# A decoder layer on one core: sums of weight panels made by accumulating DMAs in FFN-down, and panel products placed ahead of five waiting small products in the mixers

## The chip, the cores and the metric

The kernel runs on one core of a Trainium2 chip. The metric is the device time of one execution in microseconds (us), the median of several runs. The engines are named as in the profile: PE does the matrix products, ACT (ScalarE) and DVE (VectorE) the element-wise work, POOL is GpSimd, and SP only issues DMAs here.

## The reference

One layer on a residual stream of 256 tokens by 2048 channels, all in fp32. Two mixers read the normed stream through one input projection: a causal pooling mixer and an RWKV-7 time mix with 16 heads of 64. The FFN is a squared-ReLU MLP, 2048 to 8192 and back; a gated embedding and a last norm end the layer. Cut to its frame:

```python
D_MODEL, SEQ, D_FF, D_PLE, R, N = 2048, 256, 8192, 256, 1024, 64

def rms_norm(x, g):
    return x * lax.rsqrt(jnp.mean(x * x, axis=-1, keepdims=True) + 1e-6) * g

def wkv7_scan(r, decay, k, v, a_vec, b_vec):           # one head, over the 256 tokens
    def step(S, inp):
        r_t, w_t, k_t, v_t, a_t, b_t = inp
        sa = jnp.einsum('bhij,bhj->bhi', S, a_t)
        S = S * w_t[:, :, None, :] + sa[..., None] * b_t[:, :, None, :] + v_t[..., None] * k_t[:, :, None, :]
        return S, jnp.einsum('bhij,bhj->bhi', S, r_t)

def reference(x, p, ...):
    z = rms_norm(x, attn_norm) @ w_in                  # 2048 -> pool 1024, r, k, v 1024 each, w 64, a 64, g 160
    zs = token_shift(z[..., 1024:], mu_shift)          # z + (z of the token before - z) * mu
    d = causal_multiscale_pool(z[..., :1024])          # windows 2, 4, 8, 16
    pool_out = jnp.einsum('btgc,gcd->btgd', d, pool_w).reshape(B, T, 1024) * pool_scale
    rwkv_out = rwkv7_time_mix(zs, ...)                 # decay, a, g from small products; kk normed by head; the scan;
                                                       # group norm by head; + sum(r * k * r_k) * v; times g
    x = x + jnp.concatenate([pool_out, rwkv_out], -1) @ w_out
    x = x + jnp.square(jax.nn.relu(rms_norm(x, mlp_norm) @ w_ffn_up)) @ w_ffn_down
    gate = jax.nn.sigmoid(rms_norm(x, ple_norm) @ w_ple_gate)
    x = x + gate * (p @ w_ple_proj)
    return rms_norm(x, final_norm)
```

## The kernel before, in words

**Products.** Each fp32 weight panel (128 rows by 1024 columns, a 512 KB DMA that SP issues, `load_raw`) is split in two: the high half `wh` is a copy to fp32r on ACT, in two 512-wide instructions, and the low half `wl` is a subtraction on DVE, 1024 wide. An fp32 product is three matmuls with the halves (high by high, low by high, high by low), each 128x128 by 128x512 in the big stages. The activations are kept in halves too. `raw`, `wh` and `wl` tiles come from rotating pools, so a split waits until PE has read the tile that stood in its buffer.

**Order.** The program is written in one thread of calls; Tile's scheduler then orders each engine's instructions. A block under `high_priority` is placed as early as its data and buffers let it.

**The stages**, on the profile's clock: the mixers with the input and output projections to about 378 us, then the FFN in two halves of 4096 hidden channels: FFN-up 378 to 558 and FFN-down 558 to 722.5, then FFN-up 722.5 to 901 and FFN-down 901 to 1070, and the gate to the end. FFN-down is four sweeps, `d00`, `d01`, `d10`, `d11`: half by half of the output columns. A sweep adds 16 pairs of panels (`kp` 0 to 15; 256 hidden channels by 1024 columns each) into PSUM banks.

**Squares.** Most pairs are done plainly, 8 products of 128 channels by 128 tokens by 512 columns, which are 24 matmuls. Some pairs, called squares here, are done by a 2-by-2 scheme of the Strassen-Winograd kind: 7 products, 21 matmuls, for which sums of the four weight blocks (a11, a12, a21, a22 of the activations, w11 to w22 of the weights) are needed. The list `SEVEN` has seven squares in a sweep and the last sweep has four. The activations' sums are made in FFN-up (`activation_sums`, L1191); the weights' sums are made on DVE in the sweep (L1269 to L1272, four 512-wide instructions into a tile `td`), and then split: `wad` (w11, L172/L173), and 1024-wide tiles with the suffixes b, c and d (L1240 on ACT, L1241 on DVE). The products' matmuls are L1229 to L1231 (`prod`).

**Mixers.** Between the small products of the time mix stand the input projection's panel products, which are generators in a queue. `steps(n)` advances the queue by n yields (a yield is one or two matmuls), and `fill(us)` by so many us of panel products at the paces written beside the yields. A number in parentheses at a `z_...` call (for `z_zk1(1.33)`) is the same for the fill ahead of that gemm's transposes. So these numbers say how many panel matmuls PE does ahead of a small product. Small products that the change touches: `wagT` (transposes of the low-rank channels, L464), `zkT` of the second head group (transposes of `zk1s`, L498) and `kkn` (L595) behind it, `bsum` (`block_sum` in `rwkv_values`, L523), and `um` and `sm` in the loop over the four chunks c of `rwkv_core` (L854, L863). `gi` is the head group, 0 or 1.

**Norm.** `rms_stat` for the norm ahead of the FFN (`n2`) squares the residual stream in four 1024-wide ACT instructions into a tile with the tag `junk`.

Of the kernel before, what the change touches and what calls it, by code (L numbers as in the profile page):

```python
# [40 lines left out]
def trunk(  # L41
# [251 lines left out]
    def rms_stat(srcs, name):  # L293
        s4 = const.tile([128, 2, 2], F32, tag="s4", bufs=2, name=f"s4_{name}")
        for tt in range(2):
            for hf in range(2):
                junk = fp.tile([128, 1024], F32, tag="junk", bufs=1, name=f"junk_{name}{tt}{hf}")
                nc.scalar.activation(
                    junk, srcs[tt][:, hf * 1024 : (hf + 1) * 1024], AF.Square, accum_out=s4[:, tt, hf : hf + 1]
                )  # L300
# [101 lines left out]
    def head():  # L402
# [42 lines left out]
        steps(1)  # L445
# [327 lines left out]
    def rwkv_values(gi, st, zv):  # L773
# [3 lines left out]
        for tt in range(2):  # L777
# [16 lines left out]
    def rwkv_core(gi, st):  # L794
# [34 lines left out]
        for c in range(4):  # L829
# [18 lines left out]
            fill(1.59 if gi else 1.14)  # L848
# [10 lines left out]
            fill(0.72 if gi else 0.86)  # L859
# [171 lines left out]
    rwkv_k(1, st1, z_zk1(1.33))  # L1031
# [124 lines left out]
    def inv_ms():  # L1156
        ss2 = rms_stat(xr, "n2")
        nc.vector.tensor_scalar(s2, ss2, 1.0 / D, NORM_EPS, op0=ALU.mult, op1=ALU.add)
        nc.vector.reciprocal(s2, s2)

# [27 lines left out]
    SEVEN = (1, 3, 5, 7, 9, 11, 13)  # L1188
    s_slots = (0, 2, 5)

    def activation_sums(box, kp, r):  # L1191

        i = SEVEN.index(kp)
        if i % 2 == 0:
            st = a8(s_slots[i // 2], f"S{kp}", F32R) if i < 6 else fp.tile([128, 1024], F32R, tag="S", name=f"S{kp}")
            box[kp] = box[SEVEN[min(i + 1, len(SEVEN) - 1)]] = st
# [5 lines left out]
        nc.vector.tensor_tensor(s3, a11, a21, op=ALU.subtract)  # L1202
# [3 lines left out]

    def down_sweep(hf, pair, ys, sboxes, hooks=(), between=None, seven=SEVEN):

        nm = f"d{hf}{pair}"
        hooks = dict(hooks)  # L1210
# [21 lines left out]

        def halves_of(src, name, own=False):

            pool, kw = (fp, dict(bufs=2)) if own else (wp, {})
            wh = pool.tile([128, 1024], F32R, tag="graw" if own else "wh", name=f"wh_{name}", **kw)
            wl = pool.tile([128, 1024], F32R, tag="graw" if own else "wl", name=f"wl_{name}", **kw)
# [10 lines left out]
        def add(tt, c, src):  # L1248
            nc.vector.scalar_tensor_tensor(xs(tt, c), src, s2[:, tt : tt + 1], xs(tt, c), op0=ALU.mult, op1=ALU.add)

        for q, kp in enumerate(((0, 2, 1, 4, 3, *range(5, 16)) if hf else (0, 2, 1, 4, 3, 6, 5, 8, 7, 10, 9, 12, 11, 14, 13, 15)) if pair else range(16)):
# [4 lines left out]
            rx, ry = (load_raw(w_down[pair, hf * 32 + 2 * kp + i], 1024, f"{nm}_{kp}_{i}") for i in range(2))  # L1256
            if kp in seven:
# [6 lines left out]
                w11 = wa[:, 0:512], wa[:, 512:1024]  # L1264
                with tc.high_priority(20000):
                    split_sb(*w11, rx[:, 0:512])
                w21, w22 = halves_of(ry, f"{nm}_{kp}b")
                with tc.high_priority(20000):
                    nc.vector.tensor_tensor(t1, rx[:, 512:1024], rx[:, 0:512], op=ALU.subtract)  # L1269
# [220 lines left out]
```

## Time and profile before

| what | before |
|---|---|
| median of 3 runs | 1180.49 us (1180.44 to 1181.11) |
| the profiled execution | 1180.25 us, of it 1178.2 us in the span |
| granted clock | 0.998 |
| PE busy | 1162.5 us, 6419 matmuls |
| DVE busy | 873.3 us |
| ACT busy | 709.3 us |
| POOL busy | 13.7 us |
| DMA | 216.81 MB, 184 GB/s over the span |

A profile's row names an engine, a line of the kernel, an operation and its tiles (out<-in, buffer numbers left out), with its count and its time. Matmuls are pipelined: one of 128x512 shows 0.39 us, while the next starts 0.23 us behind it. In the view by instruction a bracket gives the idle time ahead of an instruction and what ended it.

### The profile page before, as it was taken

The numbers are of one execution on the slowest core, as the hardware profiler recorded it, in microseconds if no ns is written. First come the engines' busy times: TensorE is split into PE (matmuls) and PEld (weight loads), VectorE is DVE, ScalarE is ACT, GpSimd is POOL, SyncE is SP. The second block draws the span as 40 slices with busy tenths as digits, with TensorE's granted clock in tenths as the row PEclk, the third lists the DMA queues.
The fourth block names the chain that finished last, engine by engine and source line by source line (L and its number), as shares of the span: only waits on it lengthen the run. The fifth ranks groups of instructions, "written<-read, shape, count | busy, mean of one in ns | idle before, by whom it ended". The sixth has DMA issues, their size and how long they took to land.

```text
span 1178.2 us, 17287 instructions
## 1 busy us (share of the span) xinstructions
PE 1162.5 (99%) x6419; PEld 973.4 (83%) x6419; DVE 873.3 (74%) x1188; ACT 709.3 (60%) x1309; POOL 13.7 (1%) x73
## 2 busy tenths in 40 slices
PE   8999999999999999999999999999999999999997
PEld 8787777788887888888888888888888888888886
DVE  7786996964656666767988987676668879788543
ACT  7776848676545565555665664555556655568543
POOL 2100000000000000000000000000000000000000
PEclk9999999999999999999999999999999999999999
DMA  7464343354465555555556556555555555767511
GB/s 290 154 202 146 135 140 119 119 179 157 160 203 178 177 182 196 184 192 200 187 204 212 198 202 209 186 191 191 185 195 190 202 205 195 290 233 249 197 56 72
DMA packets 60756, 216.81 MB, mean 184 GB/s; under 512 B 6784, under 2 KB 7552, under 8 KB 60288
## 3 DMA queue, kind: packets, MB, share of 16 engines
q1 hardware_dynamic: 60240, 214.99, 52.5%
q8 instruction: 50, 0.82, 0.3%
q10 hardware_dynamic: 432, 0.73, 0.2%
q14 instruction: 34, 0.28, 0.1%
HBM read 213.59 MB, written 2.10 MB: 183 GB/s over the span
## 4 chain that ended last, share of the span: by engine, by line
PE 96%; ACT 1%; DVE 1%; DMA 0%; issue 0%; SPq 0%; POOL 0%; DVEq 0%; POOLq 0%
PE u_w L1112 20%; PE u_w L1117 10%; PE d_b L1231 7%; PE d_b L1229 7%; PE d_b L1230 7%; PE d_w L1231 2%; PE d_w L1229 2%; PE d_w L1230 2%; PE gt_b L242 2%; PE gt_b L241 2%; PE gt_b L238 2%; PE zk_b L241 1%; PE zk_b L242 1%; PE o_b L241 1%; PE o_b L242 1%; PE zv_b L238 1%
## 5 line engine op out<-in xcount | busy, mean ns | idle before, releaser
L1112 PE MATMUL u_w<-h,wh_u 128*128 128x512 f32 x1024 | 321.9, 395 | 0.0
L167 ACT ACTIVATE wh_u<-raw_u 128x512 fp32r<-128x512 f32 x256 | 147.5, 623 | 160.9 <-issue 98.2
L168 DVE TENSOR_TENSOR wl_u<-raw_u,wh_u 128x1024 fp32r<-128x1024 f32 x128 | 156.6, 1224 | 105.2 <-ACT wh_u L167 103.5
L1117 PEld LDWEIGHTS u_w<-h,wl_u 128*128 128x128 f32 x1024 | 192.4, 188 | 45.4
L1117 PE MATMUL u_w<-h,wl_u 128*128 128x256 f32 x1024 | 201.4, 278 | 0.0
L1112 PEld LDWEIGHTS u_w<-h,wh_u 128*128 128x128 f32 x1024 | 156.0, 189 | 0.1
L168 DVE TENSOR_TENSOR wl_gt<-raw_gt,wh_gt 128x1024 fp32r<-128x1024 f32 x24 | 29.4, 1224 | 23.2 <-ACT wh_gt L167 23.2
L167 ACT ACTIVATE wh_gt<-raw_gt 128x512 fp32r<-128x512 f32 x48 | 28.0, 638 | 23.1 <-PE gt_b L242 14.4
L241 PE MATMUL gt_b<-wh_gt,h 128*128 128x512 f32 x96 | 37.3, 389 | 0.0
L242 PE MATMUL gt_b<-wh_gt,h 128*128 128x512 f32 x96 | 37.3, 389 | 0.0
L168 DVE TENSOR_TENSOR wl_o<-raw_o,wh_o 128x1024 fp32r<-128x1024 f32 x16 | 19.6, 1222 | 12.9 <-ACT wh_o L167 9.9
L167 ACT ACTIVATE wh_o<-raw_o 128x512 fp32r<-128x512 f32 x32 | 18.4, 623 | 16.3 <-issue 8.5
L167 ACT ACTIVATE wh_zp<-raw_zp 128x512 fp32r<-128x512 f32 x32 | 18.6, 623 | 15.7 <-PE zp_b L242 7.2
L168 DVE TENSOR_TENSOR wl_zk<-raw_zk,wh_zk 128x1024 fp32r<-128x1024 f32 x16 | 19.4, 1220 | 10.4 <-ACT wh_zk L167 10.4
L241 PE MATMUL zk_b<-wh_zk,hTh 128*128 128x512 f32 x64 | 25.2, 394 | 1.4 <-ACT wh_zk L167 1.4
L241 PE MATMUL zv_b<-wh_zv,hTh 128*128 128x512 f32 x64 | 26.0, 406 | 0.0
L167 ACT ACTIVATE wh_zk<-raw_zk 128x512 fp32r<-128x512 f32 x32 | 18.4, 622 | 12.4 <-PE zv_b L242 4.0
L241 PE MATMUL zp_b<-wh_zp,hTh 128*128 128x512 f32 x64 | 25.7, 401 | 0.0
L238 PE MATMUL gt_b<-wl_gt,h 128*128 128x512 f32 x96 | 25.7, 389 | 0.0
L168 DVE TENSOR_TENSOR wl_zv<-raw_zv,wh_zv 128x1024 fp32r<-128x1024 f32 x16 | 19.4, 1218 | 8.2 <-ACT wh_zv L167 7.4
L241 PE MATMUL zr_b<-wh_zr,hTh 128*128 128x512 f32 x64 | 25.4, 397 | 0.0
L242 PE MATMUL zp_b<-wh_zp,hTl 128*128 128x512 f32 x64 | 25.0, 391 | 0.0
(840 smaller groups left out, 2963.9 us busy)
## 6 DMA issues: line engine op xcount, KB each, us to landing
raw_u<-in_w_ffn_up_dram SPq DMA_DIRECT2D x128, 512.0 KB, 3.5
raw_d<-in_w_ffn_down_dram SPq DMA_DIRECT2D x128, 512.0 KB, 4.3
raw_gt<-in_w_ple_gate_dram SPq DMA_DIRECT2D x24, 512.0 KB, 3.5
raw_zk<-in_w_in_dram SPq DMA_DIRECT2D x16, 512.0 KB, 3.7
raw_zr<-in_w_in_dram SPq DMA_DIRECT2D x16, 512.0 KB, 3.3
raw_zv<-in_w_in_dram SPq DMA_DIRECT2D x16, 512.0 KB, 3.3
raw_zp<-in_w_in_dram SPq DMA_DIRECT2D x16, 512.0 KB, 3.2
raw_o<-in_w_out_dram SPq DMA_DIRECT2D x16, 512.0 KB, 4.2
```

What stands on the lines that cost most here:

```text
L167: nc.scalar.activation(wh[:, a * 512 : (a + 1) * 512], raw[:, a * 512 : (a + 1) * 512], AF.Copy)
L168: nc.vector.tensor_tensor(wl, raw, wh.bitcast(F32), op=ALU.subtract)
L238: nc.tensor.matmul(banks[tt], ah[:, ts_], halves[a][1], start=False, stop=last)
L241: nc.tensor.matmul(banks[tt], ah[:, ts_], halves[a][0], start=i + a == 0, stop=False)
L242: nc.tensor.matmul(banks[tt], al[:, ts_], halves[a][0], start=False, stop=False)
L1112: nc.tensor.matmul(bank[:, ct, :].rearrange("p (s t) -> p s t", s=2), wh[:, cs[ct]], hl, start=k == 0, stop=False, skip_group_check=True,)
L1117: nc.tensor.matmul(bank[:, ct, 0:T], wl[:, cs[ct]], hl[:, 0, :], start=False, stop=k == 15, skip_group_check=True)
L1229: nc.tensor.matmul(banks[n], ah, wh, start=first, stop=False)
L1230: nc.tensor.matmul(banks[n], ah, wl, start=False, stop=False)
L1231: nc.tensor.matmul(banks[n], al, wh, start=False, stop=last)
```

## The change

In **FFN-down**, `SEVEN` has eight squares, and the last sweep five: 29 squares in place of 25. The panels of `w_ffn_down` lie in another order in DRAM (on the host). The sum of two weight blocks is now made by DMA: `begin_sum` has GpSimd issue a plain 256 KB DMA of one block into a slot of a two-slot tile `ring`, and then a 256 KB DMA of the other that adds to what is there (`accum_op`). The square's second panel load is 256 KB in place of 512 KB. DVE then makes the remaining sums in two instructions, of 512 and of 1024 elements. The first two sums are begun in FFN-up, and each square's end begins one further sum. The product order within a square is 1, 2, 3, 5, 6, 4, 7 (it was 1, 2, 3, 5, 7, 6, 4), and the visiting order of pairs differs in the sweeps of the second column half. Each fourth pair of split tiles has buffers of its own (`half_tiles`), `wad` lies in `junk`, and the squares of the norm's statistic in the tag `S`. Some sums have the opposite sign, so the last additions use `ns2`, the negative of `s2`.

In the **mixers**, five numbers are larger: `steps(7)` ahead of the norm and `wagT`, 1.90 for `z_zk1`, a `fill` of 0.92 ahead of `bsum` of group 0, and for chunk 0 of group 0 a fill of 1.59 ahead of `um` and one of 1.76 ahead of `sm`.

```diff
@@ rms_stat
-                junk = fp.tile([128, 1024], F32, tag="junk", bufs=1, name=f"junk_{name}{tt}{hf}")
+                junk = fp.tile([128, 1024], F32, tag="S" if name == "n2" else "junk", bufs=1, name=f"junk_{name}{tt}{hf}")
@@ head
-        steps(1)
+        steps(7)
@@ rwkv_values
+        fill(0.00 if gi else 0.92)
         bon = st["rk"]
@@ rwkv_core, chunk c
-            fill(1.59 if gi else 1.14)
+            fill(1.59 if gi or c == 0 else 1.14)
             ub = rw_bank("um")
...
-            fill(0.72 if gi else 0.86)
+            fill(0.72 if gi else 0.86 if c else 1.76)
             if c < 3:
@@ main thread
-    rwkv_k(1, st1, z_zk1(1.33))
+    rwkv_k(1, st1, z_zk1(1.90))
@@ FFN
-    SEVEN = (1, 3, 5, 7, 9, 11, 13)
+    SEVEN = (1, 3, 4, 6, 8, 9, 11, 13)
...
+        squares_of[hf, pair] = (1, 3, 6, 9, 11) if last else SEVEN
...
+    def begin_sum():
+        n = len(begun)
+        if not ring:
+            ring.append(fp.tile([128, 1024], F32, tag="S", name="ring"))
+        if n < len(in_line):
+            hf, pair, kp = in_line[n]
+            nc.gpsimd.dma_start(slot(n), w_down[pair, hf * 16 + kp, 1, :, 1, :])
+            nc.gpsimd.dma_start(slot(n), w_down[pair, hf * 16 + kp, 0, :, 1, :], accum_op=ALU.add)
+            begun.append(n)
@@ down_sweep, a square
-                t_ = a8(1, f"t{nm}_{kp}")
-                t1, t3, t2, t4 = (t_[:, c * 512 : c * 512 + 512] for c in range(4))
-                wa = fp.tile([128, 1024], F32R, tag="wa", name=f"wa{nm}_{kp}")
+                p1 = summed(hf, pair, kp)
+                t2 = p1
+                wa = fp.tile([128, 1024], F32R, tag="junk", bufs=1, name=f"wa{nm}_{kp}")
...
-                    split_sb(*w11, rx[:, 0:512])
-                w21, w22 = halves_of(ry, f"{nm}_{kp}b")
-                with tc.high_priority(20000):
-                    nc.vector.tensor_tensor(t1, rx[:, 512:1024], rx[:, 0:512], op=ALU.subtract)
-                    nc.vector.tensor_tensor(t3, ry[:, 512:1024], rx[:, 512:1024], op=ALU.subtract)
-                    nc.vector.tensor_tensor(t2, t3, rx[:, 0:512], op=ALU.add)
-                    nc.vector.tensor_tensor(t4, ry[:, 0:512], t2, op=ALU.subtract)
-                w1, w3 = halves_of(t_[:, 0:1024], f"{nm}_{kp}c")
-                w2, w4 = halves_of(t_[:, 1024:2048], f"{nm}_{kp}d", True)
+                    split_sb(*w22, ry[:, 0:512])
+                    split_sb(*w1, p1)
+                    nc.vector.tensor_tensor(t2, p1, ry[:, 0:512], op=ALU.subtract)
+                    t43 = rx.rearrange("p (r n) -> p r n", r=2)
+                    nc.vector.tensor_tensor(t43, t43, t2.unsqueeze(1).to_broadcast([128, 2, 512]), op=ALU.subtract)
+                    split_sb(*w2, t2)
+                w4, w3 = halves_of(rx, f"{nm}_{kp}d", True)
...
+                begin_sum()
@@ ffn_half
+            if f in (3, 4):
+                begin_sum()
```

The change of order, at three places. First the head of the mixers, on PE: `sbank` is the norm's sum of squares, `wagT` the transposes that need the norm, and `zk0` the panel product that runs beside them. Before:

```order
L238 MATMUL zk0_b0_216<-wl_zk0_5_487,hTh1_157 128x512
L441 MATMUL sbank_173<-ones_90,sqx1_370 128x1
L441 MATMUL sbank_173<-ones_90,sqx3_495 128x1
L441 MATMUL sbank_173<-ones_90,sqx1_370 128x1
L441 MATMUL sbank_173<-ones_90,sqx3_495 128x1
L238 MATMUL zk0_b1_217<-wl_zk0_5_487,hTh1_157 128x512
L464 MATMUL wagT_518<-ident_85,wagS_515 128x128 x2
L465 MATMUL wagT2_519<-ident_85,wagS_515 32x128
```

After:

```order
L238 MATMUL zk0_b1_217<-wl_zk0_5_487,hTh1_157 128x512
L238 MATMUL zk0_b0_216<-wl_zk0_5_487,hTh1_157 128x512
L238 MATMUL zk0_b1_217<-wl_zk0_5_487,hTh1_157 128x512
L241 MATMUL zk0_b0_216<-wh_zk0_6_517,hTh1_157 128x512
L242 MATMUL zk0_b0_216<-wh_zk0_6_517,hTl1_159 128x512
L241 MATMUL zk0_b1_217<-wh_zk0_6_517,hTh1_157 128x512
L242 MATMUL zk0_b1_217<-wh_zk0_6_517,hTl1_159 128x512
L241 MATMUL zk0_b0_216<-wh_zk0_6_517,hTh1_157 128x512
L242 MATMUL zk0_b0_216<-wh_zk0_6_517,hTl1_159 128x512
L241 MATMUL zk0_b1_217<-wh_zk0_6_517,hTh1_157 128x512
L242 MATMUL zk0_b1_217<-wh_zk0_6_517,hTl1_159 128x512
L464 MATMUL wagT_535<-ident_85,wagS_532 128x128 x2
```

Ten more panel matmuls stand between the norm's sum and `wagT`. The same place on ACT, where `rs_n1` is the square root of the norm and `wagS` the scaled copy that `wagT` transposes, one for each half of the tokens. Before:

```order
L167 ACTIVATE wh_zr0_0_584<-raw_zr0_0_582 128x512 x2
L450 ACTIVATE rs_n1_175<-sbank_173,eps_n_79 128x2
L459 ACTIVATE wagS_515<-wag_b0_169,rs_n1_175 128x288
L459 ACTIVATE wagS_515<-wag_b1_170,rs_n1_175 128x288
L335 ACTIVATE zf_176<-wagT_518,omu_154 128x256
```

After:

```order
L167 ACTIVATE wh_zr0_0_584<-raw_zr0_0_582 128x512 x2
L450 ACTIVATE rs_n1_175<-sbank_173,eps_n_79 128x2
L459 ACTIVATE wagS_532<-wag_b0_169,rs_n1_175 128x288
L167 ACTIVATE wh_zr0_1_622<-raw_zr0_1_620 128x512 x2
L459 ACTIVATE wagS_532<-wag_b1_170,rs_n1_175 128x288
L335 ACTIVATE zf_176<-wagT_535,omu_154 128x256
```

A panel's split now stands between the two halves of `wagS`. On DVE, where the reciprocal of the norm stands behind the panels' low halves, before:

```order
L144 TENSOR_SCALAR oka_155<-par_sb_77 128x8
L145 SCALAR_TENSOR_TENSOR cen_101<-jsum_92,ident_85 128x128
L168 TENSOR_TENSOR wl_zk0_7_561<-raw_zk0_7_558,wh_zk0_7_560 128x1024
L451 RECIPROCAL rs_n1_175<-rs_n1_175 128x2
L133 TENSOR_TENSOR wband_153<-wband_153,ident_85 128x128
```

After:

```order
L145 SCALAR_TENSOR_TENSOR cen_101<-jsum_92,ident_85 128x128
L168 TENSOR_TENSOR wl_zk0_6_518<-raw_zk0_6_515,wh_zk0_6_517 128x1024
L168 TENSOR_TENSOR wl_zk0_7_561<-raw_zk0_7_558,wh_zk0_7_560 128x1024
L168 TENSOR_TENSOR wl_zr0_0_585<-raw_zr0_0_582,wh_zr0_0_584 128x1024
L451 RECIPROCAL rs_n1_175<-rs_n1_175 128x2
```

One more low half, `wl_zr0_0`, stands ahead of the reciprocal. The third place is the begin of FFN-up on ACT: `h2` are the normed, transposed activations, `wh_u...` the panels of FFN-up, `junk_n2...` the squares of the norm's statistic. Before:

```order
L167 ACTIVATE wh_u00_2_3799<-raw_u00_2_3797 128x512 x2
L1140 ACTIVATE h2_3359<-h2t_3731,par_sb_77 128x256 x2
L167 ACTIVATE wh_u00_3_3822<-raw_u00_3_3820 128x512 x2
L1140 ACTIVATE h2_3359<-h2t_3731,par_sb_77 128x256 x2
L167 ACTIVATE wh_u01_0_3852<-raw_u01_0_3850 128x512 x2
L167 ACTIVATE wh_u01_1_3875<-raw_u01_1_3873 128x512 x2
```

After:

```order
L167 ACTIVATE wh_u00_2_3800<-raw_u00_2_3798 128x512 x2
L298 ACTIVATE junk_n201_4166,s4_n2_4163<-x0_2733 128x1024
L298 ACTIVATE junk_n210_4168,s4_n2_4163<-x1_2734 128x1024
L1141 ACTIVATE h2_3359<-h2t_3731,par_sb_77 128x256
L298 ACTIVATE junk_n211_4170,s4_n2_4163<-x1_2734 128x1024
L167 ACTIVATE wh_u00_3_3823<-raw_u00_3_3821 128x512 x2
L1141 ACTIVATE h2_3359<-h2t_3731,par_sb_77 128x256
L167 ACTIVATE wh_u01_0_3853<-raw_u01_0_3851 128x512 x2
L1141 ACTIVATE h2_3359<-h2t_3731,par_sb_77 128x256 x2
L172 ACTIVATE wh_d00_1b_5475<-ring_4590 128x512
L167 ACTIVATE wh_u01_1_3876<-raw_u01_1_3874 128x512 x2
```

Three of the squares, and the split of the first transferred sum (`wh_d00_1b<-ring`, a square of the first FFN-down sweep), now stand in ACT's row here. DVE's row has the matching subtraction `wl_d00_1b<-ring` ahead of `wl_u01_1`.

More of the change, by code (lines that the diff above doesn't have):

```diff
@@ L1205, in activation_sums, with slot, summed, down_sweep @@
         split_sb(st[:, 0:512], st[:, 512:1024], t_[:, 0:512])
-    def down_sweep(hf, pair, ys, sboxes, hooks=(), between=None, seven=SEVEN):
+    ring = []
+    squares_of = {}
+    visits_of = {}
+    for hf in range(2):
+        for pair in range(2):
+            last = hf + pair == 2
+            squares_of[hf, pair] = (1, 3, 6, 9, 11) if last else SEVEN
+            visits_of[hf, pair] = (0, 2, 1, 4, 3, *range(5, 16)) if last else (range(16), (0, 2, 1, 5, 3, 4, 7, 6, 10, 8, 9, 12, 11, 14, 13, 15))[pair]
+    in_line = [(*hp, kp) for hp, visits in visits_of.items() for kp in visits if kp in squares_of[hp]]
+    begun = []
+    turns = []
+    def slot(n):
+        return ring[0][:, n % 2 * 512 : n % 2 * 512 + 512]
+    def begin_sum():
[7 more added lines that the diff above has]
+            begun.append(n)
+    def summed(*square):
+        return slot(in_line.index(square))
+    def down_sweep(hf, pair, ys, sboxes, hooks=(), between=None):
         nm = f"d{hf}{pair}"
+        seven, visits = squares_of[hf, pair], visits_of[hf, pair]
         hooks = dict(hooks)
@@ L1255, in down_sweep @@
             a11, a21, a12, a22 = ((y[:, j + i * 128 : j + i * 128 + 128], y[:, 1024 + j + i * 128 : 1152 + j + i * 128]) for i in range(4))
-            rx, ry = (load_raw(w_down[pair, hf * 32 + 2 * kp + i], 1024, f"{nm}_{kp}_{i}") for i in range(2))
+            rx, ry = (panel(kp, c, f"{nm}_{kp}_{c}", 1 if c and kp in seven else 2) for c in range(2))
             if kp in seven:
```

54 lines of the change are left out of this document (32 added, 22 removed).

## The prediction

> **What bounds the kernel now.** I read the page first: PE is busy for nearly the whole span, and the chain that ended last runs on PE.
>
> ```profile
> PE 1162.5 (99%) x6419; PEld 973.4 (83%) x6419; DVE 873.3 (74%) x1188; ACT 709.3 (60%) x1309; POOL 13.7 (1%) x73
> PE 96%; ACT 1%; DVE 1%; DMA 0%; issue 0%; SPq 0%; POOL 0%; DVEq 0%; POOLq 0%
> ```
>
> So time is won by fewer matmuls, or by PE waiting less, and lost where another engine makes PE wait. The windows by stage (columns: stretch, its length, then busy time and instructions of PE, PEld, DVE, ACT, POOL, then clock, DMA share, GB/s) tell what a matmul is worth, and what stands beside it:
>
> ```profile
> 153.00:165.00 12.00, 10.99 (x58) 8.69 (x57) 11.94 (x23) 5.85 (x12) 1.08 (x2) 1.00 0.35 124
> 378.00:558.00 180.00, 179.44 (x1034) 156.65 (x1034) 124.46 (x159) 99.07 (x180) 0.00 (x0) 1.00 0.55 188
> 558.00:722.50 164.50, 164.50 (x727) 136.21 (x727) 143.51 (x163) 98.72 (x171) 0.00 (x0) 1.00 0.57 201
> 901.00:1070.00 169.00, 169.00 (x756) 139.52 (x755) 144.93 (x165) 104.94 (x188) 0.00 (x0) 1.00 0.63 226
> ```
>
> In FFN-down PE never rests: 164.50 / 727 = 0.2263 us for each matmul. DVE is next, 143.51 of 164.50, so 21 us in two sweeps are free on it. In FFN-up, one matmul in the mean takes 180 / 1034 = 0.174 us. In the mixers DVE can be fuller than PE (11.94 of 12.00). Then PE's waits, all that the view has:
>
> ```profile
> PE zk_b L241 <- ACT wh_zk L167: 1.4, 1, 1.4
> PE rbank L400 <- DVE ones L98: 1.2, 1, 1.2
> PE bsum L523 <- DVE zr_t L336: 1.0, 1, 1.0
> PE sm L863 <- ACT UV L858: 0.9, 1, 0.9
> PE wagT L464 <- POOL wband L130: 0.8, 1, 0.8
> PE zkT L498 <- ACT zk1s L488: 0.8, 2, 0.6
> PE h2t L1134 <- DVE x L1071: 0.6, 1, 0.6
> PE um L854 <- ACT R L818: 0.4, 1, 0.4
> ```
>
> Five of these are the change's places: wagT, zkT, bsum, um, sm. None lies in FFN-down, so there only the count of matmuls can gain.
>
> **FFN-down: fewer matmuls.** Four more squares, each 7 products in place of 8, three matmuls a product: 4 x 3 x 0.2263 = **-2.7 us**. That holds if DVE and ACT still keep ahead. Rows of a square before, on DVE and ACT:
>
> ```profile
> L1269 DVE TENSOR_TENSOR td<-raw_d 128x512 f32<-128x512 f32 x24 | 16.6, 691 | 1.5 <-DMA raw_d<-in_w_ffn_down_dram 0.9
> L1241 DVE TENSOR_TENSOR wl_d_1c<-td,wh_d_1c 128x1024 fp32r<-128x1024 f32 x4 | 4.9, 1220 | 0.7 <-ACT wh_d_1c L1240 0.7
> L172 ACT ACTIVATE wad<-raw_d 128x512 fp32r<-128x512 f32 x24 | 14.8, 618 | 3.7 <-DMA raw_d<-in_w_ffn_down_dram 3.7
> ```
>
> A square now has on DVE four 512-wide instructions (three low halves, one sum) and three 1024-wide (two low halves, one sum): 4 x 0.69 + 3 x 1.22 = 6.4 us, where it had 5 x 0.69 + 3 x 1.22 = 7.1. A plain pair has 2 x 1.22 = 2.4. A sweep of eight and eight is 8 x (6.4 + 2.4) = 70 us on DVE. On ACT a square has seven 512-wide copies and a pair four: 8 x 11 x 0.62 = 55. PE has 8 x (21 + 24) x 0.2263 = 81.5. PE stays the bound; if that cover were gone, each us on DVE would be one on PE. The two further sums of activations for each half, some 2 us of DVE and ACT, fall in FFN-up, where DVE is busy 124 of 180 us: nothing. The tight place is where two squares are neighbours (3, 4 and 8, 9, six times in all): the last split tiles have two buffers, so the second square's last splits start when PE has left the first. From the rows I find 0.2 to 0.7 us to spare, and take 0; the bound is 0.6 each, 3.6 in all.
>
> **FFN-down: the sums by DMA.** No GpSimd DMA and none that adds stands in the trace. The nearest rows of issue to landing, both for 256 KB, and the panels' own:
>
> ```profile
> wa<-in_wa_up_dram SPq DMA_DIRECT2D x2, 256.0 KB, 2.7
> gu<-in_g_up_dram SPq DMA_DIRECT2D x2, 256.0 KB, 4.2
> raw_d<-in_w_ffn_down_dram SPq DMA_DIRECT2D x128, 512.0 KB, 4.3
> ```
>
> The adding DMA waits for the plain one, so a sum takes 5.4 to 8.4 us by the first two rows; I take 7, in the middle. It may take as long as its slot is free. A slot serves every second square; between those lie at the least two squares and a pair on PE, (42 + 24) x 0.2263 = 14.9 us. The old sum is read last by the square's last split, some 6.4 us of DVE behind its begin, the new one some 2.5 us behind the begin of its own: 14.9 - 6.4 + 2.5 = 11 us. So 7 is hidden, by 4 us. On POOL nothing else waits behind these DMAs; on SP the panel's second load shrinks to half. If the cover is gone, each us over 11 comes to PE at up to 27 squares (29 less the two begun in FFN-up).
>
> By the Trainium skill, "DMA: Bandwidth & Descriptors", section "Anatomy of one DMA — SWDGE (gpsimd) path", such a DMA takes about 2.0 us plus its bytes at 436 GB/s, so 256 KB some 2.6 us and a sum 5.2, an estimate; by it this term is 0 as well, with 6 us to spare, and no row here shows it.
>
> **The new wait in FFN-up.** ACT now has the first sum's split in its row ahead of `wh_u01_1`, the sixth panel, and DVE likewise. Behind it are queued every further panel of FFN-up, for which PE waits.
>
> ```profile
> 377.23 1.15 ACT L167 ACTIVATE wh_u<-raw_u 128x512 fp32r<-128x512 f32 x2 [1.38 <-issue]
> 379.89 0.47 ACT L1140 ACTIVATE h<-h2t,par_sb 128x256 fp32r<-128x256 f32 x1 [1.50 <-PE h2t L1134]
> 378.71 0.69 PE L1112 MATMUL u_w<-h,wh_u 128*128 128x512 f32 x2
> L298 ACT ACTIVATE junk_n<-x 128x1024 f32<-128x1024 f32 x8 | 8.6, 1073 | 0.0
> ```
>
> The ring's tile comes free when the last square of the norm's statistic is done. On ACT these stand behind the copy that ends at 378.4: three of 1.07 us and a 0.5 us copy between, 382.1, and I add 0.5 for the start of each. From 382.6, landing is 5.4 to 8.4 us later, 388.0 to 391.0. PE starts FFN-up at 378.7 and reaches the sixth panel after five of 16 x 0.174 = 2.8 us and eight transposes of 0.11 between, at 393.5. Ahead of that lie the ring's split (0.62), the panel's copy (1.15) and its low half (1.22, needed 0.4 us late): the limit is about 390.9. I take 0, since the middle of the bounds lies 1.4 us ahead of it; bounds 0 and +2 (an issue that costs GpSimd a further us or two). The squares themselves move from a later place in FFN-up to here, 3.2 us of ACT; ACT waited 1.38 and 1.50 us there, and the last `h2` copy is needed some 1 us after it would be done: 0.
>
> **Mixers.** The rows at the five places, in time order:
>
> ```profile
> 35.93 1.15 ACT L167 ACTIVATE wh_zr<-raw_zr 128x512 fp32r<-128x512 f32 x2 [0.89 <-PE zk_b L242]
> 36.78 0.48 PE L238 MATMUL zk_b<-wl_zk,hTh 128*128 128x512 f32 x1
> 37.47 0.89 ACT L459 ACTIVATE wagS<-wag_b,rs_n 128x288 f32<-128x288 f32 x2 [0.23 <-DVE rs_n L451]
> 38.08 0.20 PEld L464 LDWEIGHTS wagT<-ident,wagS 128*128 128x128 f32 x2 [1.14 <-POOL wband L130]
> 127.65 0.39 PE L242 MATMUL zr_b<-wh_zr,hTl 128*128 128x512 f32 x1
> 128.60 0.33 PE L498 MATMUL zkT<-ident,zk1s 128*128 128x128 f32 x1 [0.56 <-ACT zk1s L488]
> 129.18 0.98 PE L498 MATMUL zkT<-ident,zk1s 128*128 128x128 f32 x7 [0.25 <-ACT zk1s L488]
> 58.06 0.64 PE L595 MATMUL kkn<-tF_t,jhead 128*32 128x256 f32 x8
> 134.64 2.13 PE L595 MATMUL kkn<-tF_t,jhead 128*32 128x256 f32 x8
> 159.46 0.30 PEld L523 LDWEIGHTS bsum<-ybuf,jsum 128*128 128x128 f32 x2 [1.17 <-PE vt L780]
> 191.64 0.86 PE L238 MATMUL zv_b<-wl_zv,hTh 128*128 128x512 f32 x3
> 192.91 0.27 PE L854 MATMUL um<-R,SC 64*64 64x64 f32 x1 [0.41 <-ACT R L818]
> 195.30 0.40 PE L242 MATMUL zv_b<-wh_zv,hTl 128*128 128x512 f32 x1
> 195.93 0.59 ACT L858 ACTIVATE UV<-um 64x512 f32<-64x512 f32 x1
> 196.57 0.69 PE L863 MATMUL sm<-UV,BKt 128*64 128x64 f32 x16 [0.88 <-ACT UV L858]
> ```
>
> - **wagT**: PE waits 1.14 us. Ten panel matmuls (2.27 us) now run first, which would hide it, but ACT and DVE are reordered too. The low half `wl_zr0_0` now ahead of the reciprocal needs a buffer that PE leaves after three matmuls from 36.78, at 37.6; with 1.22 us it ends at 38.9, the reciprocal at 39.05. Then the first `wagS` (0.45 to 0.5) to 39.6, `wh_zr0_1` (1.15, its buffer left by PE's last `wh_zk0_6` matmul at 39.4) to 40.65, the second `wagS` to 41.1. PE has nothing else from 39.3, less 0.3 for the first transposes: it waits 1.5. **+0.4** (bounds -1.1 and +0.8).
> - **zkT and kkn**: The matmul of 127.65 gives way at 127.88, so PE waits 0.72, then 0.47 (129.18 - 128.60, less the transpose itself). Three more matmuls (0.68) fill the first; the second stays, since `zk1s` does not end sooner. Behind it, `kkn` took 2.13 us where group 0's, in 58.06's row, took 0.64; it now stands later against ACT's squares of `zk`, and I take a third of the 1.5. **-1.2** (0 to -2.2).
> - **bsum**: six matmuls, 1.36 us, into a wait of 1.17: **-1.2** (0 to -1.2).
> - **um, sm**: The rows' last panel matmuls give way at 192.32 and 195.53, so PE waits 192.91 - 192.32 = 0.6 and 196.57 - 195.53 = 1.0. Three matmuls more in front of each; `UV` ends where it did, at 196.5, since ACT's row between is unchanged. Six matmuls, 1.36 us, go into waits: **-1.3** (-1.6 to 0).
>
> The panel matmuls put ahead are missing at the ends of their gemms, where the queue is simply shorter. Mixers: 0.4 - 1.2 - 1.2 - 1.3 = **-3.3**.
>
> **The sum.** -2.7 + 0 + 0 - 3.3 = -6.0. The profiled execution took 1180.25 us, so 1174.25; the median is 0.24 above it: **1174.5 us**.
>
> **The rivals.**
>
> - *All five waits go*: 1.14 + 1.19 + 1.17 + 1.6 = 5.1, and half of kkn's 1.5, so -2.7 - 5.9: **1171.9**. For it: PE's own rows have enough matmuls. Against it: the reordered reciprocal at wagT.
> - *The mixers give nothing back*: DVE is full there (11.94 of 12.00), so what PE gains at one product it waits at the next, whose inputs come no sooner. Then -2.7 alone: **1177.8**. For it: DVE stands in the chain of zr_t, kkn and bsum; against it: three waits name ACT, which is busy 5.85 of 12.00 there.
> - *The neighbouring squares stall*: +3.6, so **1178.1**.
> - *Slower: the DMA sum outlasts its slot.* If a sum takes over 11 us, the square's first split waits on ACT and DVE, then PE, at up to 27 squares. At 11.6 us it is 27 x 0.6 = 16 on top of -6.0: **1190**. It turns slower than before from 11.25 us. A way to it is that GpSimd can't write the DMA's descriptors while DVE works; DVE is busy 143.51 of 164.50. Against it: it would need 4 us more than the middle of my rows. The Trainium skill, "SBUF — State Buffer", has this as 'The "DVE blocks DMA" trap (SWDGE)': while DVE runs a two-port mode, GpSimd is locked out and the DMA waits. By that rule a sum could start only between DVE's instructions, 0.7 to 1.2 us late each time; that alone doesn't reach 11 us, and no row here shows the lock.
>
> **How the numbers follow.** Forecast 0.58, all five 0.12, nothing back 0.15, neighbours 0.05, slower 0.10. A measurement of this kernel tells about 0.2%, 2.4 us, from no change: faster is below 1178.1, which holds the first two, most of the third and half of the fourth, 0.84; same 0.06; slower 0.10. The range leaves out the slower rival and a tail at each end: 1171.5 to 1178.8.
>
> **What would show it.** In the profile after: 12 fewer matmuls; 29 sums by DMA, none over 11 us; each half's FFN-down shorter by 1.4 us (two squares more) and PE without a wait there; wagT still in the list of waits at about 1.5 us, bsum and um gone from it, sm and zkT at 0.4 to 0.5 us. The forecast is wrong if ACT or DVE wait for `ring` in FFN-down, if PE waits near 390 us, or if the mixers end less than 2 us sooner.

## The result: slower, and the profile after

| what | before | after |
|---|---|---|
| median of 7 runs each | 1180.49 us (1179.66 to 1181.53) | 1185.39 us (1183.96 to 1190.19) |
| after to before | | 1.0053, interval 1.0031 to 1.0074 |
| the profiled execution | 1180.25, span 1178.2 | 1185.39, span 1183.3 |
| PE enters FFN-up at | 378.71 us | 383.35 us |
| FFN-down, first half: first to last matmul | 164.39 us | 163.01 us |
| FFN-down, second half | 168.53 us | 167.46 us |

The forecast was 1174.5, in a range of 1171.5 to 1178.8. The kernel is slower by about 0.5%. The page of after, the engines and the chain that ended last:

```profile
PE 1162.4 (98%) x6407; PEld 971.4 (82%) x6407; DVE 878.0 (74%) x1194; ACT 713.7 (60%) x1323; POOL 56.8 (5%) x131
PE 91%; DVE 4%; ACT 2%; DMA 2%; issue 1%; SPq 0%; DVEq 0%; ACTq 0%
```

PE does the twelve matmuls fewer (6407), but is busy just as long, and PE's part of the chain fell from 96% to 91%: DVE, ACT and DMA now set the pace in places. The windows of the two FFN-down stages, cut at their matmuls (columns as in the prediction):

```profile
565.40:728.40 163.00, 163.00 (x721) 134.97 (x721) 146.57 (x162) 101.77 (x179) 23.00 (x32) 1.00 0.77 235
907.00:1074.40 167.40, 167.06 (x746) 138.16 (x745) 149.07 (x167) 106.72 (x193) 15.80 (x22) 1.00 0.77 251
```

FFN-down does what was forecast: no rest for PE in the first half, one of 0.3 us in the second (ahead of the gate), and 1.4 and 1.1 us less than before. The loss lies ahead of it. The waits of PE in after, longest first:

```profile
PE kkn L595 <- ACT tF_t L585: 2.1, 2, 1.1
PE sc L669 <- ACT UV L783: 1.5, 1, 1.5
PE sm L864 <- ACT UV L859: 1.3, 1, 1.3
PE u_w L1113 <- ACT wh_u L167: 1.3, 1, 1.3
PE rbank L400 <- DVE ones L98: 1.2, 1, 1.2
PE u_w L1118 <- DVE wl_u L168: 1.0, 1, 1.0
PE wag_b L393 <- ACT wagh L379: 0.9, 1, 0.9
PE wagT L464 <- ACT wagS L459: 0.9, 1, 0.9
```

`bsum` left the list, as planned, but `kkn`, `sc` and two matmuls of FFN-up (`u_w`) entered it, and `sm` waits longer. With the stages this gives the span: +4.6 in the mixers, +2.9 in the first FFN-up, -1.4 and -1.1 in the two FFN-down stages, together +5.0 of the 5.1. One execution of the mixers is good to 1 or 2 us only: in the five traces whose mixers are those of before, PE enters FFN-up between 377.72 and 380.14.

**The clock.** The granted clock tells a second part:

| kernel | runs | with a mean clock of 0.998 or more | median of these | median of the rest |
|---|---|---|---|---|
| before (beside the experiments) | 91 | 62 | 1180.1 us | 1181.5 us |
| after | 7 | 2 | 1184.0 us | 1189.5 us |

So at full clock the change costs some 4 us, and it makes executions with a lower clock more frequent. (In every trace the clock is 0.50 for the last 3 to 6 us, where PE has next to nothing to do. The nine of the fourteen traces with a mean of 0.998 or more have no other drop; the five with 0.996 or less have one or two.) Where the clock fell in the profiled one shows in the windows around `kkn` (the column after POOL is the clock):

```profile
133.00:137.00 4.00, 1.91 (x10) 0.89 (x10) 3.90 (x10) 2.70 (x7) 0.00 (x0) 1.00 0.40 130
137.00:141.00 4.00, 3.95 (x12) 2.03 (x13) 3.53 (x12) 3.67 (x7) 0.00 (x0) 0.57 0.64 231
```

PE is busy 1.91 of the first 4 us, and in the next 4 the clock is 0.57 in the mean: it is 0.50 for 3.41 us, from 137.15, and full around that. At half the clock PE loses at most half of 3.41, 1.7 us, and the mean over the execution falls by 0.0014 (estimates from these numbers). The traces with the mixers of before agree: the three without a drop enter FFN-up at 377.72 to 378.71, and the two that have one, at 38.1 and 38.6 us (the late split and the plain second DMA), at 379.87 and 380.14. By the same sum the three runs of after at 0.994, some 6 us over the two at 0.998, had about three drops each (an estimate too).

### The profile page after: what moved, and what is told of

It is laid out like the page before. It is cut to its first block, busy times and chain, and to the rows that moved or that the text cites. A ratio compares the mean times of both kernels' runs of the same rounds, so it can differ in the third digit from the quotient of the medians.

```text
span 1183.3 us, 17405 instructions
## 1 busy us (share of the span) xinstructions
PE 1162.4 (98%) x6407; PEld 971.4 (82%) x6407; DVE 878.0 (74%) x1194; ACT 713.7 (60%) x1323; POOL 56.8 (5%) x131
## 4 chain that ended last, share of the span: by engine, by line
PE 91%; DVE 4%; ACT 2%; DMA 2%; issue 1%; SPq 0%; DVEq 0%; ACTq 0%
PE u_w L1113 19%; PE u_w L1118 10%; PE d_b L1261 7%; PE d_b L1262 7%; PE d_b L1263 7%; PE d_w L1263 2%; PE d_w L1261 2%; PE d_w L1262 2%; PE gt_b L238 2%; PE gt_b L241 2%; PE gt_b L242 2%; PE o_b L241 1%; PE o_b L242 1%; PE o_b L238 1%; PE zr_b L241 1%; PE zr_b L238 1%
## 5 line engine op out<-in xcount | busy, mean ns | idle before, releaser
L1231 POOL DMA_DIRECT2D ring<-in_w_ffn_down_dram x29 | 16.6, 574 | 622.8 <-DVE r L1357 190.5
L172 ACT ACTIVATE wad<-ring 128x512 fp32r<-128x512 f32 x29 | 18.2, 628 | 43.5 <-DVE ring L1312 43.5
L1314 DVE TENSOR_TENSOR raw_d<-raw_d,ring 128x1024 f32<-128x1024 f32 x29 | 35.5, 1222 | 0.7
L1232 POOL DMA_DIRECT2D ring<-in_w_ffn_down_dram x29 | 25.2, 869 | 101.5 <-DMA ring<-in_w_ffn_down_dram 101.5
L168 DVE TENSOR_TENSOR wl_zv<-raw_zv,wh_zv 128x1024 fp32r<-128x1024 f32 x16 | 19.5, 1221 | 10.8 <-ACT wh_zv L167 10.8
```

The lines of the kernel that those rows point to most:

```text
L168: nc.vector.tensor_tensor(wl, raw, wh.bitcast(F32), op=ALU.subtract)
L1232: nc.gpsimd.dma_start(slot(n), w_down[pair, hf * 16 + kp, 0, :, 1, :], accum_op=ALU.add)
L1314: nc.vector.tensor_tensor(t43, t43, t2.unsqueeze(1).to_broadcast([128, 2, 512]), op=ALU.subtract)
```

## The experiments: which part loses, and why

The theory from the two traces had three parts: (a) each panel product that is put ahead drags work of DVE or ACT, or a PSUM bank, ahead of the next small product, so PE waits there; (b) the first sum lands too late for FFN-up; (c) FFN-down gains 2.7 us. The rivals: the sums by DMA slow the sweeps, the clock alone makes the difference, or 29 squares are not worth their extra work. Each run was timed in 3 or 5 rounds against before, on one of three chips, and the ratio is to before on the same chip. Before's median was 1180.23 us beside the FFN part alone, the mixer part alone, the late split and zk1 alone; 1180.27 beside the other single numbers and zk1 with the held low half; and 1180.75 beside the bank, the plain second DMA, the fewer squares and the whole change with the late split.

### The FFN part alone

The five mixer numbers are those of before:

```diff
-        steps(7)
+        steps(1)
-        fill(0.00 if gi else 0.92)
-            fill(1.59 if gi or c == 0 else 1.14)
+            fill(1.59 if gi else 1.14)
-            fill(0.72 if gi else 0.86 if c else 1.76)
+            fill(0.72 if gi else 0.86)
-    rwkv_k(1, st1, z_zk1(1.90))
+    rwkv_k(1, st1, z_zk1(1.33))
```

> The changed kernel with the five mixer numbers of before. Theory A (the mixers lost 4.6 us by reordered splits; in FFN-up the first sum's split made every panel behind it wait for the DMA, 2.7 us; FFN-down itself gained 2.7): mixers end as before, PE waits about 2.7 us in FFN-up's sixth panel, total 1180.5 us, the same as before. Rival B (the sums by DMA cost time all over the sweeps, by traffic or by DVE locking GpSimd out): over 1182 us, with waits of ACT and PE in FFN-down. Rival C (the first sum's wait comes only with the mixers' delay): 1178.

Measured: 1182.56 us (12 runs, 1180.01 to 1184.29), ratio 1.0015 [1.0007, 1.0023]. The FFN part alone doesn't gain either. The waits of PE in this kernel's FFN-up:

```profile
PE u_w L1112 <- ACT wh_u L167: 1.8, 1, 1.8
PE u_w L1117 <- DVE wl_u L168: 1.0, 1, 1.0
```

These waits show 2.8 us, and FFN-up as a whole is longer by more: 182.5 us from its first to its last matmul, against 179.1 in before. These 3.4 us take the 2.7 that FFN-down gives. The median lies in rival B's range, but its mechanism isn't there: PE's list of waits names none in FFN-down, and FFN-down has its gain. The next experiment but one tests that.

### The mixer part alone

Before, with the five numbers of the change.

> The kernel before with the five mixer numbers of the change. Theory A: FFN-up starts 4.6 us later than before, so about 1185 us, and the granted clock falls near 138 us. Rival B (the mixers lose nothing by themselves): 1177 to 1180.

Measured: 1184.91 us (6 runs), 1.0042 [1.0027, 1.0057]. The mixers lose 4.7 us by themselves, 3.9 at full clock, and this trace too has the drop of the clock, from 137.3 us.

### The FFN part, with the first sum's split late

A one-element copy from the last part of FFN-up's activations into the split's tile is put ahead of the first sum's split. The tile then can't be written before FFN-up's end, and the split leaves the place ahead of the sixth panel:

```diff
                 w22, w1 = ((wh[:, c : c + 512], wl[:, c : c + 512]) for c in (0, 512))
+                if in_line.index((hf, pair, kp)) == 0:
+                    nc.scalar.activation(wh[:, 512:513], ys[7][:, 0:1].bitcast(F32), AF.Copy)
                 with tc.high_priority(20000):
```

> FFN part alone, and ahead of the first sum's split a one-column copy from the last hidden tile of the half, so that the split can't stand in FFN-up's first panels. Theory A: the 2.7 us wait goes, 12 matmuls fewer remain: 1177.8 us, 2.7 below before. Rival B (sums by DMA cost in the sweeps): no better than the FFN part with the early split.

Measured: **1177.84 us** (9 runs, 1176.89 to 1178.76), 0.9975 [0.9965, 0.9985], and no wait of PE in FFN-up or FFN-down. This version beats both kernels. FFN-up takes 179.1 us again. Against the FFN part alone it gains 4.7 us at the median and 2.9 at full clock (1180.1 to 1177.2, of 3 and 4 runs): that is near the 3.4 us of FFN-up. The rest goes with the clock, which was 0.998 or more in 3 of 12 runs with the wait and in 4 of 9 without it.

Why the split came late is in after's chain around 391 us (start, time taken, what):

```profile
386.77 0.19 ACT junk_n L298
386.96 0.53 ACT wh_u L167
387.49 0.12 issue
387.61 3.16 DMA ring<-in_w_ffn_down_dram
390.77 0.29 issue
391.06 7.33 DMA ring<-in_w_ffn_down_dram
398.40 0.02 issue
398.42 0.02 ACT wh_d_1b L172
...
398.96 1.14 ACT wh_u L167 x2
400.12 1.24 DVE wl_u L168
401.36 0.04 issue
401.40 0.50 PE u_w L1118 x2
```

The sum took 398.40 - 387.61 = 10.8 us, of which the adding DMA 7.3. Behind it, in ACT's row, stood the panel `wh_u`, and PE waited for that. The durations of all 29 sums stand in the view of the two DMA lines of after, the plain one (L1231) and the adding one (L1232):

```profile
L1231 POOL DMA_DIRECT2D ring<-in_w_ffn_down_dram x29: 563/567/711, 387.6 to 1020.7; - x29
...
DMA to landing us min/median/max: 2.8/3.6/5.9
```
```profile
L1232 POOL DMA_DIRECT2D ring<-in_w_ffn_down_dram x29: 853/867/893, 391.1 to 1026.9; - x29
...
who waited for it (us, times):
  ACT wh_d_1b L172: 5.8, 1
...
DMA to landing us min/median/max: 3.9/6.2/8.1
```

The median pair, with what lies between the two DMAs, takes 10.8 us (7.2 to 13.1). Yet only one sum of 29 was waited for. The two sums of FFN-up are begun one behind the other, so their adding DMAs run at the same time (391.06 to 398.40 and 392.39 to 399.83).

### The FFN part with a plain second DMA

Is it the adding that is slow? Here the second DMA is a plain one too:

```diff
-            nc.gpsimd.dma_start(slot(n), w_down[pair, hf * 16 + kp, 0, :, 1, :], accum_op=ALU.add)
+            nc.gpsimd.dma_start(slot(n), w_down[pair, hf * 16 + kp, 0, :, 1, :])
```

> The FFN part with the early split, the second DMA of each sum written plainly over the first instead of added to it (the sums are then left out of the result). If adding is what makes the pair take 10.8 us: the pair falls to 7 to 7.5 us as the prediction had it, the first sum lands at about 390, PE's wait in FFN-up falls from 2.8 us to under 0.5, total 1177.5 to 1178.5. If it is GpSimd's issue or the traffic of FFN-up: the pair stays over 10 us and the time at 1182.

Measured: 1178.35 us (11 runs), 0.9978 [0.9970, 0.9987]. The second DMA, now plain, and its one waiter, in this kernel's view of that line:

```profile
L1231 POOL DMA_DIRECT2D ring<-in_w_ffn_down_dram x29: 536/536/550, 387.8 to 1020.5; - x29
...
  ACT wh_d_1b L172: 3.0, 1
...
DMA to landing us min/median/max: 2.9/5.1/6.5
```

The median falls from 6.2 to 5.1, so adding costs about 1.1 us. The plain DMA in the second place still takes about 1.5 more than the first (5.1 against 3.6); no run shows why. The first pair landed after 8.0 us, where the FFN part alone has 11.3, and the median pair after 9.2 in place of 10.8, so not the 7 to 7.5 us that were expected. PE had no wait in FFN-up, though ACT still waited 3.0 us: the limit is sharp, and this sum met it.

### Fewer squares

The FFN part with the late split, and 25 squares as before.

```diff
-            squares_of[hf, pair] = (1, 3, 6, 9, 11) if last else SEVEN
+            squares_of[hf, pair] = (1, 3, 6, 9) if last else (1, 3, 6, 8, 9, 11, 13)
```

> The FFN part with the late first split, but 7, 7, 7, 4 squares as before: transferred sums without the further squares. Theory A (only the count of matmuls gains): 1180.5, as before, 2.7 us over the run with 29 squares. Rival (the transferred sums themselves gain or lose): other than 1180.5 by over 1 us.

Measured: 1180.16 us (11 runs), 0.9998 [0.9989, 1.0006]. Its FFN-down stages take 164.35 and 168.43 us, before's times to 0.1. So the sums by DMA bring nothing by themselves; the whole gain of the FFN part is the four more squares. Whether 29 squares would gain as much with their sums made on DVE, as before, was not run.

### One mixer number at a time

Before, with one of the changes each: `steps(7)`; `z_zk1(1.90)`; the fill of 0.92 ahead of `bsum`; the two chunk-0 fills ahead of `um` and `sm`.

> The kernel before with steps(7) alone. By the prediction +0.4 us; by the trace of the changed kernel, where the second transposes of the first k stood 0.3 us sooner, -0.3: 1179.9 to 1180.6, no change that can be told.

> The kernel before with 1.90 in place of 1.33 ahead of the second group's transposes. Theory A (a panel's low half on DVE moves ahead of the shifted k that kkn waits for; PE then idles some 3 us and the clock drops): zrT 2 to 3 us later than before, granted clock about 0.6 near 138 us, total 1182 to 1183.5. Rival B (what kkn loses comes from the other four numbers): 1179.5 to 1180.5.

> The kernel before with the fill ahead of bsum alone. By the prediction: -1.2, 1179.0. By the theory of reordered engines: bsum's wait goes, but the score products behind it wait for the copies of the vt bank on ACT (1.7 us in the changed kernel), so 1180 to 1181.

> The kernel before with the two chunk-0 fills alone. Here ACT's row between R and UV has the same instructions as before, unlike in the changed kernel, where a 1.06 us tmp copy came in. By that: sm's and um's waits shrink to 0.3 us in sum, -1.3, total 1179.0. Rival (the displaced panels make later chunks wait as much): 1180.2.

| part | median | ratio | new or longer wait of PE | gone |
|---|---|---|---|---|
| `steps(7)` | 1180.47 us | 0.9999 [0.9990, 1.0008] | `wagT`, 0.9 for `wagS` and 0.3 for `wband` (before: 0.8) | none |
| `z_zk1(1.90)` | 1182.33 us | 1.0014 [1.0005, 1.0023] | `kkn`, 2.4 in three waits | 0.6 of `zkT`, 0.6 of `bsum` |
| fill of `bsum` | 1184.47 us | 1.0033 [1.0022, 1.0044] | `sc` 1.7 and 0.4, `sm` 1.2 (before: 0.9) | `bsum` 1.0 |
| `um` and `sm` | 1181.40 us | 1.0010 [1.0001, 1.0020] | `rym`, 1.2 | 0.7 of `sm`, 0.2 of `um` |

No part gains, and three lose. By the ratios they lose 0, 1.7, 3.9 and 1.2 us, together 6.7, where the five numbers in one kernel lost 4.7 to 5.0. At full clock (runs at 0.998 or more, against those of before on the same chip) they lose 0.5, 1.5, 2.2 and 1.3 us alone, and 3.9 in one kernel, so the clock isn't what makes the sums differ. Only `steps(7)` and the zk1 part came out in the ranges expected, and zk1's trace has no drop of the clock and `zrT` only 0.9 us later; the fill of `bsum` lost over 3 us more than either theory gave it, and `um` and `sm` lost where a gain or no change was expected.

**zk1.** Three more panel matmuls stand ahead of `zkT`. In after, which has the same edit, DVE's instructions there are (start, time, then what):

```profile
133.60 0.27 DVE L724 TENSOR_TENSOR X<-X,AT 128x108 f32<-128x108 f32 x1
133.79 0.87 DVE L336 SCALAR_TENSOR_TENSOR zk_t<-zkT,par_sb,zk_t 128x255 f32<-128x255 f32 x2
134.57 1.22 DVE L168 TENSOR_TENSOR wl_zr<-raw_zr,wh_zr 128x1024 fp32r<-128x1024 f32 x1
135.71 0.87 DVE L336 SCALAR_TENSOR_TENSOR zk_t<-zkT,par_sb,zk_t 128x255 f32<-128x255 f32 x2
```

In before the last `zk_t` starts at 134.85, and the same low half stands behind it:

```profile
134.85 0.47 DVE L336 SCALAR_TENSOR_TENSOR zk_t<-zkT,par_sb,zk_t 128x255 f32<-128x255 f32 x1
...
136.65 1.23 DVE L168 TENSOR_TENSOR wl_zr<-raw_zr,wh_zr 128x1024 fp32r<-128x1024 f32 x1
```

The low half of the next panel, 1.22 us, now cuts the four `zk_t` in two. ACT has made that panel's high half by 130.2 in after; in before the second part of it began only at 136.0, behind the squares. ACT's squares `tF_t` need `zk_t`, and `kkn` needs `tF_t`. DVE is busy 3.90 of 4 us there, so there is no room that would hide it.

**um and sm.** The `UV` that `sm` waits for comes nearly in time here (a wait of 0.2 us). But on DVE the same happens one step later, in the kernel with this part alone:

```profile
205.37 1.22 DVE L168 TENSOR_TENSOR wl_zv<-raw_zv,wh_zv 128x1024 fp32r<-128x1024 f32 x1
206.70 0.86 DVE L874 TENSOR_TENSOR sbd<-sbd,sm 64x256 f32<-64x256 f32 x2
```

A low half of 1.22 us starts ahead of the state's update `sbd`; in before `sbd` starts at 205.98 and the low half at 207.78. `rym` of the third chunk waits the 1.2 us.

**bsum.** The six matmuls fill their wait. But the small products share a pool of four PSUM banks (`rw_bank`), and with the fill the second block of `sc` waits for ACT's `UV`, which is read out of `vt`'s bank: it seems to get that bank, free only when ACT has made `UV` from it. A trace doesn't name banks; an experiment below tests this. After's ACT and PE there:

```profile
174.75 2.13 ACT L743 ACTIVATE SC<-X 32x1024 f32<-32x1024 f32 x2 [2.74 <-DVE X L739]
...
177.32 1.19 ACT L783 ACTIVATE UV<-vt 64x512 f32<-64x512 f32 x2
```
```profile
176.55 0.48 PE L669 MATMUL sc<-AR,BK 64*128 64x128 f32 x2
178.56 1.16 PE L669 MATMUL sc<-AR,BK 64*128 64x128 f32 x14 [1.53 <-ACT UV L783]
```

In before the second block starts at 173.83, ahead of `UV` (175.40), so it has another bank there. Why the fill changes the hand-out is not shown. The same fill also changes ACT's row ahead of `sm` in after:

```profile
198.51 1.06 ACT L709 ACTIVATE tmp<-SC 32x1024 f32<-32x1024 f32 x1
199.59 1.16 ACT L167 ACTIVATE wh_zv<-raw_zv 128x512 fp32r<-128x512 f32 x2
200.77 1.06 ACT L710 ACTIVATE tmp<-tmp 64x1024 f32<-64x1024 f32 x1
201.85 0.59 ACT L859 ACTIVATE UV<-um 64x512 f32<-64x512 f32 x1
```

`tmp<-SC` (1.06 us) did not stand between `R` and `UV` in before. So `UV` comes later by that much against `R`, which is more than the fill ahead of `sm` adds. It stands there with the fill of `bsum` alone too, and not with the `um` and `sm` fills alone.

### Taking each cause away

For zk1, the low half that cuts in is held back on DVE until the last `zk_t`:

```diff
-            nc.vector.tensor_tensor(wl, raw, wh.bitcast(F32), op=ALU.subtract)
+            if name == "zr1_3":
+                with tc.issue_after(shifted[-1].ins):
+                    nc.vector.tensor_tensor(wl, raw, wh.bitcast(F32), op=ALU.subtract)
+            else:
+                nc.vector.tensor_tensor(wl, raw, wh.bitcast(F32), op=ALU.subtract)
```

> The run with 1.90 alone, and DVE's low half of zr1's fourth panel held behind the last of the four shifted k. Theory A (DVE's order sets kkn): the last two zk_t come 1.2 us sooner, PE's waits for kkn fall from 2.4 to about 1.2 us, total 1180.5 to 1181. Rival (the inverse's steps alone on DVE set it): no change against 1.90 alone, 1182.3.

Measured: 1180.76 us (11 runs), 1.0005 [0.9996, 1.0014]; `kkn` waits 1.0 in place of 2.4. That gives back most of the loss, but makes no gain: the wait that zk1 removes at `zkT` is there again at `kkn`. In this trace the first `zk_t` starts at 133.88, and in before at 132.81. Seven steps of the inverse (`X`, 0.3 us each) stand on DVE between the low half ahead of it and it; in before there are three. So the rival has a part too: what is left of the wait is these steps. In the program a `fill` also advances the inverse (`pace`).

For bsum, the second `vt` takes its bank from the other set:

```diff
-            b = rw_bank("vt")
+            b = mm_bank("vt") if gi == 0 and tt == 1 else rw_bank("vt")
```

> The fill ahead of bsum alone, with the second vt bank taken from the other PSUM pool, so that no score product waits for the vt copies on ACT. Theory A (the fill changed which bank the second score block gets, one that ACT frees late): the score wait of 1.7 us and the clock dip behind it go, 1184.5 falls to 1179.5 to 1181; the sm wait of 1.2 us stays. Rival (the score products wait for their data on ACT and DVE anyway): still over 1183.

Measured: nine runs between 1180.99 and 1184.64 us, 1183.17 in the middle, ratio 1.0020 [1.0010, 1.0030] (a tenth run, at 3473.54 us, is left out; its cause isn't known). That is the rival's range. The wait for `UV` at `sc` is gone, and another stands there:

```profile
PE sc L669 <- DVE SC L676: 1.3, 1, 1.3
PE sm L864 <- ACT UV L859: 1.2, 1, 1.2
```

So the bank is shown for the wait itself, but by the ratios for less than half of the 3.9 us (0.9 of 2.2 at full clock); behind it stands DVE, nearly as late as ACT was, and `sm` waits as before this edit.

Last, all of the change with the late split of the first sum:

> The whole change with the late first split: if the terms add, the mixers' loss of 4.7 us and FFN-down's gain of 2.7 stay: 1182.3. If the two waits share a cost (the clock), further off than 1 us.

Measured: 1182.34 us (10 runs), 1.0013 [1.0002, 1.0024]. Against the FFN part with the same split (0.9975) the mixers cost 0.38%, 4.5 us. This profile is the control for the clock, since its windows around `kkn` have the wait without the drop:

```profile
133.00:137.00 4.00, 1.94 (x11) 0.72 (x9) 3.88 (x10) 2.98 (x8) 0.00 (x0) 1.00 0.39 137
137.00:141.00 4.00, 3.71 (x19) 2.56 (x16) 3.77 (x11) 3.97 (x8) 0.00 (x0) 1.00 0.67 237
```

PE does 19 matmul instructions in the second 4 us, where after did 12. With nearly the same waits ahead of FFN-up it enters FFN-up at 381.26, and after at 383.35; of the 2.1 us between them the drop explains at most 1.7. This execution was the fastest of its ten.

## Why the prediction was wrong, by its steps

- **Fewer matmuls, -2.7: right.** -2.4 at the median with the late split, and 0.23% (2.7 us) between 29 and 25 squares. The neighbouring squares cost nothing, as taken.
- **Sums hidden in the sweeps, cost 0: right, on a wrong margin.** The term "I take 7, in the middle" was mis-sized: 10.8. The bounds came from two rows of plain DMAs on SP; neither the adding (1.1 us more) nor a second place behind the first was in them. The first DMA came as taken (3.6 us at the median); the second was the mis-sized one (6.2). Ten of the 29 sums took over 11 us, where the forecast had none; their splits stood 12.3 us or more behind the begin, so nothing waited. The slot estimate of 11 us held: from a sum's begin to its split lie 9.9 to 12.5 us in after's first sweep. So the "4 us" to spare were nearly none: inside a sweep the sums landed 0.03 to 3.8 us ahead of their split where squares lie close together, the tightest at 624.73 for a split at 624.76.
- **"The new wait in FFN-up ... I take 0": wrong, by the same 7.** The begin of the sum was right: forecast at 382.6, it began at 387.61, which less the 4.64 us by which FFN-up started later is 383.0. The limit of 390.9 was right too. In after it is 395.5, the sum landed at 398.40, 2.9 late, and FFN-up took 2.9 us longer than in before. In the FFN part alone the limit is 389.9 and ACT's split began at 393.30, 3.4 late, and FFN-up took 3.4 longer. With the plain second DMA the limit is 392.3, the sum landed at about 392.3, and FFN-up took no longer. So the step that failed here is the landing time alone.
- **Mixers, -3.3: wrong in sign, +4.7 (3.9 at full clock).** Two steps failed. "`UV` ends where it did, since ACT's row between is unchanged" was not so: an instruction of 1.06 us came into that row. And for zkT and bsum I counted the matmuls that go into a wait and took the product's own inputs as unmoved; I did not follow what the earlier panel matmuls set free on DVE (the low half of 1.22 us ahead of `zk_t`), which steps of the inverse come with them, and which PSUM bank the next small product then gets. "I take a third of the 1.5" at kkn, a gain of 0.5, was a wait of 2.1 to 2.4. But for wagT's, the bounds were 0 at worst, and nothing in the trace excluded a loss. At wagT the forecast of a longer wait (+0.4) was near: 1.2 in two waits in after, by `wagS` and `wband`, from 0.8.
- **The clock: not in the prediction at all.** At full clock after takes 1184.0 us, 3.9 more than before; its median is a further 1.4 above.

Of the rivals, "the mixers give nothing back" had the mechanism ("what PE gains at one product it waits at the next"), but priced it at nothing gained. The slower rival named the sums by DMA, in the wrong place: in the sweeps no sum outlasted its slot, and the one that came late was the first, in FFN-up. Its port lock, which the Trainium skill has ("SBUF — State Buffer", 'The "DVE blocks DMA" trap (SWDGE)'), isn't seen: the adding DMA that took 7.3 us ran in FFN-up, where DVE is busy 4.67 us in the 12 from 390, while the median of all 29, nearly all in the sweeps, where DVE is busy 146.57 of 163.00 us, is 6.2. That speaks against the lock for these DVE instructions, but weakly, since the two adding DMAs of FFN-up ran at the same time; no run here tested it by itself. The estimate of 2.6 us for a DMA of 256 KB, worked out from the Trainium skill ("DMA: Bandwidth & Descriptors", "Anatomy of one DMA — SWDGE (gpsimd) path"), doesn't agree with the traces: the plain one took 3.6 us at the median, the adding one 6.2.

**What stays open.** Why the four mixer parts lose 6.7 us alone and 4.7 to 5.0 together was not settled; one lost wait can cover another. In bsum's 3.9 us, the bank, DVE's later work and the clock are told apart only roughly. Why a DMA in the second place takes longer isn't known. That the waits bring on the clock's drops is a match of places and of counts, not shown by a run that has the one without the other's cause.

## What to carry to other kernels

A panel product put ahead of a waiting small product is free only if what it sets free (the next panel's low half, its copies, the PSUM bank) is not placed ahead of the small product's own chain; on an engine as full as DVE was here (3.90 of 4 us) the wait moved one product on and grew. So follow the order on the engines behind the move to the next two small products before you count the wait as won, and hold the released instruction back if it cuts in, which here gave back most of the loss and no more. A consumer that waits for a transfer is best kept out of an engine's row ahead of work that PE needs soon: moving one split made a loss of 0.15% a gain of 0.25%.

## What the runs showed of the hardware

A GpSimd DMA that adds 256 KB to what is in the tile took 6.2 us at the median (3.9 to 8.1), the plain one ahead of it 3.6 (2.8 to 5.9), and a plain one in the adding one's place 5.1.

The granted clock fell to 0.50 for 3.41 us in after, behind 4 us in which PE was idle for some 2, in pieces of about 1 us; with nearly the same waits it fell in one execution and not in another. In the bsum part alone it was 0.50 for twice that, 6.83 us from 176.44, behind the waits of `sc` (the windows mix it with full clock):

```profile
172.00:176.00 4.00, 2.54 (x12) 1.64 (x10) 3.00 (x4) 3.12 (x5) 0.00 (x0) 1.00 0.57 190
176.00:184.00 8.00, 7.37 (x30) 5.82 (x32) 3.65 (x4) 4.92 (x12) 0.00 (x0) 0.57 0.26 91
```

The Trainium skill, "TensorE: Matmul & The Clock Gate", section "What's actually happening", says that the gate watches an activity window of about 3.4 us that runs freely, so that the same kernel can come out differently in each run. The traces agree with that: the drops last 3.41 us or twice that, and the one behind `kkn` is in after and not in the last experiment. Its section "HAM oscillation — how this bites in real kernels" has as the abstract rule that PE's idle gaps should stay under some 3.4 us; here the six drops in the traces came behind waits of at most 0.5 to 1.7 us each, and the wait of 1.8 us in the FFN part alone was followed by none.
